# Layer 0's bias from the positional encoding, taken from the prompt's own compression

## The chip, the cores and the metric

The kernel runs on one core of a Trainium2 chip. The metric is the device time of one execution in microseconds; the time before is the median of three runs. Names of engines: PE is TensorE (PEld its weight loads), DVE is VectorE, ACT is ScalarE, POOL is GpSimd, SP is SyncE, which issues most DMAs.

## What is computed

One inference step of a decoder trunk of two layers, for one prompt of 256 new tokens and eight sequences with 8 new tokens and 1024 old ones each; all 320 tokens go through the same weights. A layer mixes tokens by three paths (a state-space path, a causal pooling, and sparse attention), projects, and runs a convolutional feed-forward block. The change lies in the sparse attention, where keys and values are compressed in blocks of 32 rows, 16 apart:

```python
def compress_blocks(rows, pe, w1, w2):
    ...
    ch = rows.reshape(b, n_ch, CMP_STRIDE, d)
    h = (jnp.einsum('bnld,lde->bne', ch[:, :-1] + pe[:CMP_STRIDE], w1[:CMP_STRIDE])
         + jnp.einsum('bnld,lde->bne', ch[:, 1:] + pe[CMP_STRIDE:], w1[CMP_STRIDE:]))
    return jax.nn.gelu(h) @ w2
```

The encoding `pe` adds the same vector of 128 numbers to every block, `sum over l, d of pe[l, d] * w1[l, d, :]`, once for keys and once for values. The kernel computes that vector once per layer and uses it as the bias of the Gelu. The prompt has 15 blocks per layer, the eight sequences have 63 each from their cache.

## The kernel before

The kernel is written with a framework that sorts the program: each engine executes its instructions in an order that is fixed when the program is built, from the instructions' priorities (their place in the program) and from when their inputs are ready in the framework's own plan. `later(n)` adds n to the priorities of what stands in it, so that it yields to others. At run time every engine takes its queue strictly as it is written, and waits by semaphores. Tiles come from pools with a fixed number of buffers; a tile is freed when its last reader is done.

Layer 0's mixing part is listed in `ORDER[0]`, one short name per stage, with `@n` for `later(n)`. Those that matter here: `lw` loads the weights of the compression (`w1`, two tiles of 128 x 2048, and `w2`, which also holds `pe` in the columns 128 to 159). `hP0` and `hP2` gather cache pages with 32 indirect DMAs that POOL issues. `eb` is `enc_bias`, the stage that is dropped. `pr` is `nsa_prep`, which transposes the prompt's keys, values and queries and compresses its 15 blocks. `x` is `xbc`, eight tiles of the input projection (24 matmuls `mt` each, weights split in two parts by ACT and DVE, results taken over by DVE into `ext`, edge columns copied to `ocv`). `c0` to `c3` compress the sequences' cache (`cs`).

`enc_bias` (line 834) takes `pe` as the stationary operand: 16 matmuls for keys and 16 for values, each of 32 stationary columns (only the first is wanted) against 128 columns of `w1`, in four groups of 32 partitions of the tile `pe`. Each is written in two passes in the trace. ACT copies the sums to `pes`, two small matmuls `hb` add up the four groups, and DVE copies the two columns to `c.hb`. Layer 1 runs the same stage in `feed`, between the layers.

`nsa_prep` compresses the prompt in the same manner. `pcl` holds the prompt's rows, 16 chunks for each of eight pairs of rows, for keys and values; 32 matmuls `pc` with 32 stationary columns each run against `w1`, into four groups of partitions. Of the 32 result rows 15 are used. DVE copies them to `pcs`; the matmuls `pf` add up the four groups with a constant (`FOLD`) and turn the result; ACT applies the Gelu with bias `c.hb` into `hc`; `ckp` and `cvp` apply the second weight. `cvp` needs `hpd`, a copy of `hc` that POOL makes.

Of the kernel before, what the change touches and what calls it, by code (L numbers as in the profile page):

```python
# [7 lines left out]
_o = 0  # L8
for _n, _w in (("ID", 128), ("ONE", 128), ("P", 1), ("TRI", 128), ("TRIU", 128), ("TRIS", 64), ("TRIUS", 64), ("GM", 128), ("SEL", 256), 
               ("CAU", 128), ("CMP", 32), ("HS", 12), ("NEW", 8), ("WOLD", 8), ("COS", 24), ("SIN", 24), ("RW", 2),  # L10
               ("IC", 32), ("FOLD", 15), ("J1", 14), ("BM", 4), ("B8", 8)):
    globals()["C_" + _n] = _o
    _o += _w
NCST = _o
# [11 lines left out]
def constants():  # L26
    f = np.float32
    c = np.zeros((128, NCST), f)
    p = np.arange(128)
    c[:, C_ID:C_ID + 128] = np.eye(128)  # L30
    c[:, C_ONE:C_ONE + 128] = 1
    c[:, C_P] = p
    c[:, C_TRI:C_TRI + 128] = p[:, None] <= p[None]
    c[:, C_TRIU:C_TRIU + 128] = p[:, None] > p[None]
    q = np.arange(64)
    same = q[:, None] // 8 == q[None] // 8
    c[:64, C_TRIS:C_TRIS + 64] = same & (q[:, None] <= q[None])
    c[:64, C_TRIUS:C_TRIUS + 64] = same & (q[:, None] > q[None])
    same_bq = (p[:, None] // 32 == p[None] // 32) & (p[:, None] % 8 == p[None] % 8)
    c[:, C_GM:C_GM + 128] = same_bq  # L40
    for g in range(2):
        b, h, i = p // 32 + 4 * g, p // 8 % 4, p % 8
        c[b * 8 + i, C_SEL + 128 * g + p] = 1
    c[:, C_HS:C_HS + 12] = (p // 8 % 4)[:, None] == np.arange(12)[None] // 3
    c[:, C_CAU:C_CAU + 128] = np.where(p[None] <= p[:, None], 0, NEG)
    for qt in range(2):
        m = np.where(16 * np.arange(16)[None] + 31 <= (qt * 128 + p)[:, None], 0, NEG)
        m[:, 15] = NEG
        c[:, C_CMP + 16 * qt:C_CMP + 16 * qt + 16] = m
    c[:, C_NEW:C_NEW + 8] = np.where(np.arange(8)[None] <= (p % 8)[:, None], 0, NEG)  # L50
    c[:, C_WOLD:C_WOLD + 8] = np.where(np.arange(8)[None] > (p % 8)[:, None], 0, NEG)
    half = 8
    inv = (1.0 / (f(500000.0) ** (np.arange(half, dtype=f) / f(half)))).astype(f)
    for j in range(3):
        pos = (p + 128 * j if j < 2 else 1024 + p % 8).astype(f)
        ang = (pos[:, None] * inv).astype(f)
        c[:, C_COS + 8 * j:C_COS + 8 * j + 8] = np.cos(ang)
        c[:, C_SIN + 8 * j:C_SIN + 8 * j + 8] = np.sin(ang)
    for g, w in enumerate((2, 4, 8, 16)):
        r = slice(64 * (g % 2), 64 * (g % 2) + 64)  # L60
        c[r, C_RW + g // 2] = f(1) / f(w)
        c[r, C_IC + 16 * (g // 2):C_IC + 16 * (g // 2) + 16] = f(w) / np.minimum(np.arange(16) + 1, w).astype(f)
    c[:, C_FOLD:C_FOLD + 15] = (p % 32)[:, None] == np.arange(15)[None]
    c[:, C_J1:C_J1 + 14] = np.arange(1, 15)
    c[:96, C_BM:C_BM + 4] = (p[:96] % 32)[:, None] // 8 == np.arange(4)[None]
    c[:64, C_B8:C_B8 + 8] = q[:, None] // 8 == np.arange(8)[None]
    return c
# [71 lines left out]
def post(o):  # L139
# [28 lines left out]

ORDER = ["lw hP0@500 hP2@500 eb@100 hS1@500 pr x hS3 st g c0@0 c1 p0 c2 c3@200 l0 o0 n0@200 p1 o1 s0 po n1@0 z l1 s1@0 r0@100 r1@100 ss",
         "pr n0 st l0@500 g@500 n1 p0 p1 z s0@0 o1 po r0 l1@500 o0 s1@100 x r1 ss"]  # L170


def build(ctx, tc, nc, A):
# [4 lines left out]
    F32, F32R, I32 = mybir.dt.float32, mybir.dt.float32r, mybir.dt.int32  # L178
    AF, OP = mybir.ActivationFunctionType, mybir.AluOpType
    X, XY = mybir.AxisListType.X, mybir.AxisListType.XY  # L180
    PE, DVE, ACT, POOL, SP = nc.tensor, nc.vector, nc.scalar, nc.gpsimd, nc.sync
# [35 lines left out]
    s1 = pool("s1", 1)  # L217
# [58 lines left out]
    cst = one.tile([128, NCST], F32, name="cst")  # L276
# [5 lines left out]
    def mm(out, l, r, start=True, stop=True):  # L282
        return PE.matmul(out, l, r, start=start, stop=stop, skip_group_check=True)  # L283
# [537 lines left out]
    def load_w1(c):  # L821
        c.w2 = s1.tile([128, 416], F32, name="w2", tag="w2")
        SP.dma_start(c.w2, A["w2"][c.l])
        ck = s1.tile([128, 4, 80], F32, name="ckT", tag="ckT")
        c.ckT = [ck[0:64], ck[64:128]]
        c.cvb = [s1.tile([80, 4, 64], F32, name="cvb", tag=f"cvb{g}") for g in range(2)]
        c.w1 = []
        for kv in range(2):
            w = w8_p.tile([128, 16, 128], F32, name="w1", tag="w8")
            SP.dma_start(w, A["w1"][c.l, kv].rearrange("p (k c) -> p k c", k=16))  # L830
            c.w1.append(w)
# [42 lines left out]
    def nsa_prep(c):  # L874
        l, kvn, qn = c.l, c.kvn, c.qn
        pcl = n2([128, 512], "pcl")
        POOL.memset(pcl[:, 256:288], 0.0)
        pv = pcl[:, 0:256].rearrange("p (i k c) -> p i k c", i=2, k=8)
        c.KT = KT = s1.tile([64, 528], F32, name="KT", tag="KT")
        c.qT = [n2([64, 4, 128], "qT") for _ in range(2)]  # L880
        kvd = n2([128, 2, 2, 2, 64], "kvd")
        qd = n2([64, 4, 2, 64], "qd")
        for u in range(2):
            ACT.activation(kvd[:, :, :, u], kvn[:, 0:2, 0:128].rearrange("p j (i d) -> p j i d", i=2), AF.Copy)
            DVE.tensor_copy(qd[:, :, u], qn[2][:64].rearrange("p (h d) -> p h d", h=4))
        for j in range(2):
            ps = nst("kT")
            for i in range(2):
                transpose(ps[:, 128 * i:128 * i + 128], kvd[:, j, i].rearrange("p u d -> p (u d)"))
            transpose(ps[:64, 256:384], kvn[:, j, 128:192])  # L890
            transpose(ps[:64, 384:512], kvn[:, j, 256:320])
            for i in range(2):
                for par in range(2):
                    r = slice(64 * par, 64 * par + 64)
                    v = ps[r, 128 * i:128 * i + 128].rearrange("p (c k u) -> p k c u", k=8, u=2)[:, :, :, par]
                    cp(f"pv{l}{j}{i}{par}", "A" if par else "D", pv[r, i, :, 8 * j:8 * j + 8], v)
            cp(f"KT{l}{j}", "A", KT[:, 272 * j:272 * j + 256], ps[:64, 256:512])
            ps = nst("qT")
            for h in range(4):
                transpose(ps[:64, 128 * h:128 * h + 128], qn[j][:, 64 * h:64 * h + 64])  # L900
            cp(f"qT{l}{j}", "A", c.qT[j], ps[:64].rearrange("p (h t) -> p h t", h=4))
        hc = n1("hc")[:, :64].rearrange("p (v k) -> p v k", v=2)
        POOL.memset(hc, 0.0)

        ps = nst("pc")
        for kv in range(2):
            for kk in range(16):
                r, c0 = 32 * (kk % 4), 128 * kv + 16 * (kk % 8) + kk // 8
                mm(ps[r:r + 32, 128 * kv:128 * kv + 128], pcl[:, c0:c0 + 32], c.w1[kv][:, kk], start=kk < 4, stop=kk > 11)
        pcs = d1("pcs")  # L910
        cp(f"pcs{l}", "D", pcs, ps[:, 0:256])
        ps = nst("pf")
        for kv in range(2):
            mm(ps[:, 16 * kv:16 * kv + 15], pcs[:, 128 * kv:128 * kv + 128], cst[:, C_FOLD:C_FOLD + 15])
            ACT.activation(hc[:, kv, 0:15], ps[:, 16 * kv:16 * kv + 15], AF.Gelu_apprx_tanh, bias=c.hb[:, kv:kv + 1])
        ps = nst("ckp")
        mm(ps[:64, 0:16], c.w2[:, 0:64], hc[:, 0, 0:16])
        DVE.tensor_copy(KT[:, 256:272], ps[:64, 0:16])
        ps = nst("cvp")
        hpd = n1("hpd").rearrange("p (h k) -> p h k", h=4)  # L920
        POOL.tensor_copy(hpd, hc[:, 1:2, :].to_broadcast([128, 4, 32]))
        mm(ps[:, 0:64], hpd.rearrange("p h k -> p (h k)"), c.w2[:, 64:128])
        c.cvd = s1.tile([128, 4, 64], F32, name="cvd", tag="cvd")
        POOL.memset(c.cvd, 0.0)
        for h in range(4):
            r = slice(32 * h, 32 * h + 32)
            DVE.tensor_copy(c.cvd[r, h], ps[r, 0:64])

        c.qsT = s1.tile([128, 8, 4, 8], F32, name="qsT", tag="qsT")
        ps = nst("qsT")  # L930
        for h in range(4):
            transpose(ps[:, 64 * h:64 * h + 64], qd[:, h].rearrange("p u d -> p (u d)"))
        ACT.activation(c.qsT.rearrange("p b h q -> p h b q"),
                       ps[:, 0:256].rearrange("p (h b q) -> p h b q", h=4, b=8), AF.Copy)
        c.nT = A_p.tile([128, 2, T], F32, name="nT", tag="A")
# [333 lines left out]
    c = params(0)  # L1269
# [61 lines left out]
```

## Time and profile before

| | |
|---|---|
| median of three runs | 1232.06 us (1231.94 to 1237.4) |
| the profiled execution | 1224.47 us, its span 1222.3 us |
| PE | 1171.7 us busy, 96% |
| DVE / ACT / POOL | 66% / 44% / 25% busy |
| granted clock of PE | 0.97 on average |

The span is the time from the first to the last instruction of the profiled execution. Layer 0's mixing part ends at about 235 us, its output projection at 265 us, its feed-forward block at 630 us; layer 1's mixing part lies between 650 and 815 us. A matmul's end is modelled, so neighbouring matmuls overlap in the listing: the distance from one start to the next is what a matmul costs.

### The profile page before, as it was taken

What the parts mean: (1) busy time and instruction counts of PE and PEld (TensorE: products, weight loads), DVE (VectorE), ACT (ScalarE), POOL (GpSimd) and SP (SyncE); (2) the same over time, 40 slices, a digit from 0 to 9 for tenths busy, and PEclk for the clock granted to TensorE, in tenths of its full rate; (3) what the DMA queues carried; (4) which work ended last, traced back from release to release, by engine and by line L of the source; (5) the groups of instructions that cost most, each with busy time, mean ns of one, the idle gap of its engine ahead of it and who ended that gap; (6) DMA issues with size and microseconds to landing.
All of it is one profiled execution on the core that took longest, in us unless ns stands there. A gap on an engine that the chain in (4) does not pass through costs nothing.

```text
span 1222.3 us, 23199 instructions
## 1 busy us (share of the span) xinstructions
PE 1171.7 (96%) x8450; PEld 1093.2 (89%) x8450; DVE 802.5 (66%) x1661; ACT 536.7 (44%) x950; POOL 302.5 (25%) x616
## 2 busy tenths in 40 slices
PE   7999998899999999999999999889999999999995
PEld 6799765599999999999999877778899999999995
DVE  4583667368756666656663688986685666666665
ACT  5445523236454444433433565433455444444431
POOL 4732222100513113311300033440342311111111
PEclk9999999699999999999999999898899999999998
DMA  7634227355555455545433445206345544445421
GB/s 277 191 100 137 76 85 252 100 161 185 175 177 199 167 168 181 159 146 184 156 104 105 154 131 189 99 27 199 119 138 171 165 143 159 152 145 158 150 72 43
DMA packets 85186, 180.18 MB, mean 147 GB/s; under 512 B 10449, under 2 KB 45009, under 8 KB 84049
## 3 DMA queue, kind: packets, MB, share of 16 engines
q1 hardware_dynamic: 84048, 176.61, 45.0%
q0 software_dynamic: 1024, 2.10, 0.6%
q8 instruction: 66, 1.08, 0.4%
q14 instruction: 48, 0.39, 0.1%
HBM read 168.97 MB, written 13.83 MB: 150 GB/s over the span
## 4 chain that ended last, share of the span: by engine, by line
PE 88%; DVE 5%; POOL 2%; ACT 2%; issue 1%; DMA 1%; SPq 1%; DVEq 0%; POOLq 0%; ACTq 0%
PE mt L283 67%; PE cs L283 5%; PE nat L283 4%; PE sn L283 1%; PE O L283 1%; PE sb L283 1%; PE sc L283 1%; PE yoh L283 1%; PE ss L283 1%; PE pe L283 1%; PE rb L283 1%; PE pT L287 1%; DMA h<-s_ssm 1%; PE sA L283 1%; DVE xt L437 1%
## 5 line engine op out<-in xcount | busy, mean ns | idle before, releaser
L342 ACT ACTIVATE wh<-raw 128x1024 fp32r<-128x1024 f32 (+2 forms) x156 | 159.9, 1026 | 199.7 <-PE mt L283 147.2
L283 PE MATMUL mt<-xh,wa 128*128 128x320 f32 x1024 | 237.2, 310 | 0.0
L283 PE MATMUL mt<-xl,wh 128*128 128x320 f32 x736 | 232.0, 315 | 0.0
L283 PE MATMUL mt<-xh,wl 128*128 128x320 f32 x736 | 231.2, 314 | 0.0
L283 PE MATMUL mt<-xh,wh 128*128 128x320 f32 x736 | 230.9, 315 | 0.2 <-ACT xh L421 0.2
L290 DVE TENSOR_TENSOR wl<-raw,wh 128x1024 fp32r<-128x1024 f32 (+2 forms) x151 | 179.5, 1189 | 68.2 <-ACT wh L342 65.5
L283 PEld LDWEIGHTS mt<-xh,wa 128*128 128x128 f32 x1024 | 174.8, 188 | 0.3
L283 PE MATMUL mt<-xl,wa 128*128 128x320 f32 x512 | 158.5, 310 | 0.0
L283 PEld LDWEIGHTS mt<-xh,wh 128*128 128x128 f32 x736 | 138.9, 189 | 5.8 <-issue 5.0
L283 PEld LDWEIGHTS mt<-xh,wl 128*128 128x128 f32 x736 | 138.8, 189 | 4.6 <-issue 3.9
L283 PEld LDWEIGHTS mt<-xl,wh 128*128 128x128 f32 x736 | 139.0, 189 | 3.2 <-issue 2.4
L290 DVE TENSOR_TENSOR wa<-raw,wa 128x1024 fp32r<-128x1024 f32 x92 | 113.5, 1234 | 37.2 <-ACT wa L342 36.9
L290 POOL TENSOR_TENSOR fa<-fa,fc 128x256 f32<-128x256 f32 (+1 forms) x128 | 82.0, 662 | 191.5 <-ACT fc L1171 136.8
L342 ACT ACTIVATE wa<-raw 128x1024 fp32r<-128x1024 f32 x92 | 96.8, 1053 | 48.4 <-DMA raw<-wg 34.9
L283 PE MATMUL mt<-act,wa 128*128 128x320 f32 x768 | 117.8, 309 | 0.0
L283 PEld LDWEIGHTS mt<-act,wa 128*128 128x128 f32 x768 | 114.0, 188 | 0.0
L283 PE MATMUL mt<-act,wh 128*128 128x320 f32 x512 | 113.2, 309 | 0.0
L283 PEld LDWEIGHTS mt<-xl,wa 128*128 128x128 f32 x512 | 96.3, 188 | 0.0
L1164 POOL COPY off<-fext 128x2 f32<-128x2 f32 x64 | 19.5, 304 | 283.2 <-DVE fext L290 283.2
L283 PEld LDWEIGHTS mt<-act,wh 128*128 128x128 f32 x512 | 85.6, 188 | 0.0
L290 DVE TENSOR_TENSOR fo<-fo,mt 128x320 f32<-128x320 f32 x112 | 54.0, 484 | 44.6 <-PE mt L283 44.3
L283 PE MATMUL mt<-act,wl 128*128 128x320 f32 x256 | 79.1, 309 | 0.0
(375 smaller groups left out, 1976.2 us busy)
## 6 DMA issues: line engine op xcount, KB each, us to landing
raw<-wg SPq DMA_DIRECT2D x168, 512.0 KB
raw<-wd SPq DMA_DIRECT2D x64, 512.0 KB
cache<-cslc SPq DMA_DIRECT2D x128, 64.0 KB
cache<-ccmp SPq DMA_DIRECT2D x96, 64.0 KB
w<-w SPq DMA_DIRECT2D x4, 1024.0 KB
o_sss<-h SPq DMA_DIRECT2D x16, 256.0 KB
o_winold<-wnat SPq DMA_DIRECT2D x16, 252.0 KB
raw<-wnb SPq DMA_DIRECT2D x8, 384.0 KB
```

Of the source, the lines that this page charges most:

```text
L283: return PE.matmul(out, l, r, start=start, stop=stop, skip_group_check=True)
L287: return PE.transpose(out, in_, ident[:k, :k])
L290: return eng.tensor_tensor(out, a, b, op)
L342: ACT.activation(h, src, AF.Copy)
L437: DVE.scalar_tensor_tensor(t, mixo[k], w(k), rb if k else pb, op0=OP.mult, op1=OP.mult)
L1164: POOL.tensor_copy(off[:, m % 8, 0:2], ext[:, 256:258])
```

## The change

In layer 0 the stage `eb` is dropped from the order. `pcl` gets 32 columns for each pair of rows in place of 16, is set to zero as a whole, and POOL copies the encoding from `w2` into its columns 16 and 17. The `pc` matmuls, as many as before, then compute the encoding's sum as a 17th result row. The fold takes 17 columns instead of 15. Where no bias is there yet (layer 0), DVE copies it out of the fold's result, and the two Gelus follow behind both folds. In layer 1 `enc_bias` still runs, and the 17th row is computed and not used.

```diff
-               ("IC", 32), ("FOLD", 15), ("J1", 14), ("BM", 4), ("B8", 8)):
+               ("IC", 32), ("FOLD", 17), ("J1", 14), ("BM", 4), ("B8", 8)):
...
-ORDER = ["lw hP0@500 hP2@500 eb@100 hS1@500 pr x hS3 st g c0@0 c1 p0 c2 c3@200 l0 o0 n0@200 p1 o1 s0 po n1@0 z l1 s1@0 r0@100 r1@100 ss",
+ORDER = ["lw hP0@500 hP2@500 hS1@500 pr x hS3 st g c0@0 c1 p0 c2 c3@200 l0 o0 n0@200 p1 o1 s0 po n1@0 z l1 s1@0 r0@100 r1@100 ss",
...
+        c.hb = None
...
         pcl = n2([128, 512], "pcl")
-        POOL.memset(pcl[:, 256:288], 0.0)
-        pv = pcl[:, 0:256].rearrange("p (i k c) -> p i k c", i=2, k=8)
+        POOL.memset(pcl, 0.0)
+        pv = pcl.rearrange("p (i k c) -> p i k c", i=2, k=8)
+        for i in range(2):
+            POOL.tensor_copy(pv[:, i, :, 16:18], c.w2[:, 128 + 16 * i:144 + 16 * i].rearrange("p (u k) -> p k u", u=2))
...
-                r, c0 = 32 * (kk % 4), 128 * kv + 16 * (kk % 8) + kk // 8
-                mm(ps[r:r + 32, 128 * kv:128 * kv + 128], pcl[:, c0:c0 + 32], c.w1[kv][:, kk], start=kk < 4, stop=kk > 11)
+                r, c0 = 32 * (kk % 4), 256 * kv + 32 * (kk % 8) + kk // 8
+                w = min(32, 512 - c0)
+                mm(ps[r:r + w, 128 * kv:128 * kv + 128], pcl[:, c0:c0 + w], c.w1[kv][:, kk], start=kk < 4, stop=kk > 11)
...
         for kv in range(2):
-            mm(ps[:, 16 * kv:16 * kv + 15], pcs[:, 128 * kv:128 * kv + 128], cst[:, C_FOLD:C_FOLD + 15])
-            ACT.activation(hc[:, kv, 0:15], ps[:, 16 * kv:16 * kv + 15], AF.Gelu_apprx_tanh, bias=c.hb[:, kv:kv + 1])
+            mm(ps[:, 18 * kv:18 * kv + 17], pcs[:, 128 * kv:128 * kv + 128], cst[:, C_FOLD:C_FOLD + 17])
+        if c.hb is None:
+            c.hb = s1.tile([128, 2], F32, name="hb", tag="hb")
+            DVE.tensor_copy(c.hb, ps[:, 16:36:18])
+        for kv in range(2):
+            ACT.activation(hc[:, kv, 0:15], ps[:, 18 * kv:18 * kv + 15], AF.Gelu_apprx_tanh, bias=c.hb[:, kv:kv + 1])
```

## Rows read from the trace of the kernel before

**Rows 1.** The page's engine totals: busy us, share of the span, instructions.
```profile
PE 1171.7 (96%) x8450; PEld 1093.2 (89%) x8450; DVE 802.5 (66%) x1661; ACT 536.7 (44%) x950; POOL 302.5 (25%) x616
```

**Rows 2.** Busy time by stretch: length, PE, PEld, DVE, ACT, POOL, clock, DMA share, GB/s.
```profile
60.00:65.00 5.00, 3.72 (x22) 3.30 (x22) 2.68 (x8) 1.60 (x3) 2.70 (x8) 0.87 0.24 67
65.00:70.00 5.00, 5.00 (x32) 5.00 (x32) 4.27 (x10) 2.17 (x5) 1.13 (x1) 0.79 0.28 96
...
130.00:140.00 10.00, 10.00 (x50) 6.80 (x50) 8.97 (x26) 2.30 (x6) 8.26 (x12) 1.00 0.40 118
...
220.00:230.00 10.00, 4.84 (x14) 2.16 (x14) 1.68 (x3) 1.26 (x2) 1.55 (x2) 0.50 0.24 79
230.00:240.00 10.00, 10.00 (x58) 8.85 (x57) 5.56 (x24) 2.40 (x8) 0.55 (x2) 0.78 0.30 88
```

**Rows 3.** Timeline of PE around the dropped stage: start us, us, instruction.
```profile
37.86 0.41 PE L283 MATMUL pe<-w,w 128*32 128x128 f32 x2
38.19 0.42 PE L283 MATMUL mt<-xh,wl 128*128 128x320 f32 x1
...
38.87 0.41 PE L283 MATMUL mt<-xh,wh 128*128 128x320 f32 x1
...
46.69 1.28 PE L283 MATMUL pe<-w,w 128*32 128x128 f32 x34
47.90 0.42 PE L283 MATMUL mt<-xh,wh 128*128 128x320 f32 x1
...
49.94 0.28 PE L283 MATMUL hb<-cst,pes 128*128 128x1 f32 x2
```

**Rows 4.** PE's timeline: prompt's compression, a later gap; brackets: idle before, its releaser.
```profile
54.08 1.95 PE L283 MATMUL pc<-w,pcl 128*32 128x128 f32 x64
...
57.59 0.36 PE L283 MATMUL pf<-cst,pcs 128*128 128x15 f32 x2 [0.64 <-DVE an L556]
...
59.79 0.29 PE L283 MATMUL pf<-cst,pcs 128*128 128x15 f32 x2
...
62.50 0.43 PE L283 MATMUL cvp<-w,hpd 128*128 128x64 f32 x2 [1.28 <-POOL hpd L921]
...
227.00 1.92 PE L283 MATMUL yoh<-h,csp 128*32 128x256 f32 x4 [5.16 <-DMA h<-s_ssm]
```

**Rows 5.** Timeline of POOL, from the start to the copy hpd.
```profile
1.43 0.13 POOL L877 MEMSET pcl<- 128x32 f32 x1
...
18.68 0.10 POOL L328 MEMSET ms<- 128x3 f32 x1 [4.43 <-DVE rt L305]
18.96 1.18 POOL L469 DMA_INDIRECT cache<-ccmp,idx  x1 [0.17 <-issue]
...
59.95 0.94 POOL L469 DMA_INDIRECT cache<-ccmp,idx  x1 [0.30 <-issue]
...
61.12 0.52 POOL L196 COPY ocv<-ext 128x3 f32<-128x3 f32 x1
...
62.16 0.28 POOL L921 COPY hpd<-hc 128x128 f32<-128x128 f32 x1
...
84.65 0.21 POOL L196 COPY ocv<-ext 128x24 f32<-128x24 f32 x1 [2.29 <-DVE ext L290]
```

**Rows 6.** The chain that ended last, in order of time: start us, us, what.
```profile
68.55 17.01 PE mt L283 x116
```

**Rows 7.** Timeline of DVE: the second tile's weights, the first tile's result, the old bias.
```profile
37.39 1.28 DVE L290 TENSOR_TENSOR wl<-raw,wh 128x1024 fp32r<-128x1024 f32 x1
...
46.80 0.56 DVE L290 TENSOR_TENSOR ext<-mt,rb 128x256 f32<-128x256 f32 x2 [5.42 <-PE mt L283]
...
52.52 0.14 DVE L846 COPY hb<-hb 128x2 f32<-128x2 f32 x1
```

**Rows 8.** Timeline of SP: the load of w2.
```profile
9.16 0.33 SPq L823 DMA_DIRECT2D w<-w  x1
```

**Rows 9.** Timeline of POOL in layer 1, ahead of the copy hpd there.
```profile
689.81 0.29 POOL L290 TENSOR_TENSOR anb<-an,cst 64x64 f32<-64x64 f32 x1 [28.49 <-DVE an L556]
```

More of the change, by code (lines that the diff above doesn't have):

```diff
@@ L62, in constants @@
         c[r, C_IC + 16 * (g // 2):C_IC + 16 * (g // 2) + 16] = f(w) / np.minimum(np.arange(16) + 1, w).astype(f)
-    c[:, C_FOLD:C_FOLD + 15] = (p % 32)[:, None] == np.arange(15)[None]
+    c[:, C_FOLD:C_FOLD + 17] = (p % 32)[:, None] == np.arange(17)[None]
     c[:, C_J1:C_J1 + 14] = np.arange(1, 15)
```

## The prediction

> **What bounds the kernel now.** I read four views, in this order. The engine totals say that TensorE (PE) is occupied for 96% of the span and POOL for a quarter [rows 1]; a kernel like this gains where PE's own work shrinks, and only there. The table by stretch then says where that is true: from 70 us to 140 us PE has no idle time in any row (the last one stands there), and the last stretch of layer 0 before the output projection (220 to 230 us) is no longer a matter of PE work, as PE is occupied there for 4.84 of 10 us [rows 2]. Third, PE's own timeline around the stage that is dropped [rows 3], and around the prompt's compression that takes the work over [rows 4]. Last, POOL's queue, because one PE instruction behind the compression waits for POOL [rows 4, 5]. The reader should see two things. The dropped stage lies in PE's queue with no gap, so its time is PE time. And POOL's queue is closed from 18.96 us to 60.89 us by 32 gathers that are issued one by one every 1.25 us [rows 5].
>
> **The removed stage.** The 64 records of `pe` (32 matmuls of 32 columns, two passes each) lie between 37.86 us and the `hb` at 49.94 us, and are interleaved with the x tiles' matmuls `mt`: 13 times one `mt` and one pair of `pe`, then 34 records of `pe` in a row, then two more pairs [rows 3]. An `mt` in an undisturbed row costs 17.01/116 = 0.147 us [rows 6]. One step of the interleaving, from one `mt` to the next, takes 38.87 - 38.19 = 0.68 us, so a pair costs 0.68 - 0.147 = 0.53 us; in a row, 34 records take 1.21 us (46.69 to 47.90), 0.036 us each. The stage's price on PE is 15 pairs x 0.53 + 1.21 = 9.2 us. The two visits of `hb` are listed with 0.28 us, which overlaps their neighbours; I take half, 0.14 us each. Sum removed: 9.5 us. The copy `pes` on ACT and the old `hb` copy on DVE go too; DVE idles for 5.42 us in this stretch, until the first x tile is ready [rows 7], and ACT waits for the same tile, so they count as nothing. Layer 1 keeps its stage.
>
> The Trainium skill, TensorEngine Tiling (Array Packing), section Tiling Modes, says that narrow tiles run side by side, but that a change of tiling mode drains the engine. By the first half alone the stage would be worth 64 x 0.036 = 2.3 us, by both halves some 9 us; the rows agree with both halves.
>
> **What takes its place on PE.** The compression of the prompt already issues 32 stationary blocks of 32 columns (`pc`, 64 records, 1.95 us) [rows 4]. Rows 16 of these blocks were computed before and thrown away; filled with the encoding they cost nothing more. The last block is 31 columns wide; nearest rows are the 32-column ones, so 0, at most one switch (0.53 us). The fold is 17 columns for 15: 0. Both folds now stand before both Gelus: before, the second fold waited for the first Gelu, 2.2 us behind the first one [rows 4]. The new copy of the bias stands between fold and Gelu on DVE: 0.14 us by its own old row [rows 7] and one handover more. So this chain is as long as before, within 1 us on either side, and I take 0.
>
> **POOL.** The memset of `pcl` grows from 32 to 512 columns: 0.13 us becomes at most 16 times that, 2.1 us; it stands at 1.43 us, and the gathers can't start before the instruction at 18.68 us, ahead of which POOL has 4.43 us of idle time: 0 [rows 5]. The two new copies have 16 columns each; copies of 24 and of 3 columns take 0.21 and 0.52 us, so both cost 0.4 to 1.0 us; I take 0.5 us, nearer to the row with more columns. Their input, the load of `w2`, is issued at 9.16 us [rows 8], and POOL's idle time ahead of 18.68 us comes behind that [rows 5]: there they cost nothing. If the order puts them between the gathers, the gathers end 0.5 us later. I take 0.3 us. In layer 1 POOL is idle for 28.49 us ahead of that place [rows 9]: 0, unless something on PE is reordered there (bounds -1 and +1 us).
>
> **Where the freed 9.5 us go.** Behind the compression stands `cvp`, which waits for POOL's copy `hpd` [rows 4]. `hpd` runs at 62.16 us, directly behind the gathers [rows 5]. It isn't late by its input: even the copy of the first x tile's edge (`ocv`), whose input was ready at 47.36 us [rows 7], stands behind all 32 gathers. `hpd` needs the chain kT, pcl, pc, pf, hc, which the order sets after that first tile, so I expect it to stay behind the gathers. The gathers start after an instruction that waits for the first norm (18.68 us) and do not depend on the dropped stage. So `cvp` stays at 62.5 us, plus the 0.3 us. PE gains only as far as it has done other work before `cvp`.
>
> That other work is x tiles. The second tile's matmuls begin at 47.90 us, though their weights were split by 38.67 us [rows 3, 7]. And the 34 `pe` records in a row stand exactly between the last `mt` of one tile and the first of the next: some 17 instructions of the program lie between these two, and 17 `pe` matmuls were merged in, one per place. So the order is made by place in the program, not by lack of work, and a place that `pe` leaves is taken by an `mt`. With one `mt` for each of the 32 `pe` matmuls, PE has 32 x 0.147 = 4.7 us of later work done when it stands before `cvp`, and 9.5 - 4.7 = 4.8 us are given back as a longer wait there (1.28 us before). Both ends stay for the range: no `mt` more (0 gained) and all of 9.5 us.
>
> **The clock.** Around the 1.28 us before `cvp` the granted clock falls: the stretches 60 to 65 and 65 to 70 us have 0.87 and 0.79, a mean of full speed (2.4 GHz) and the lower of the two levels (1.2 GHz) [rows 2, 4]. That costs 5 x 0.13 + 5 x 0.21 = 1.7 us. Behind the 5.16 us gap at 227 us [rows 4] the clock is at 0.50 up to 230 us and 0.78 in the 10 us after it [rows 2]: (230 - 227) x 0.5 + 10 x 0.22 = 3.7 us. A wait of some 6 us before `cvp` thus costs between -1.7 us (no fall) and 3.7 - 1.7 = 2.0 us more than before; I take 1.0 us, nearer to the second row as its gap is nearer.
>
> The Trainium skill, TensorE: Matmul & The Clock Gate, section Why this matters for your kernels, says that idle gaps between bursts of matmuls bring the clock back to its lower level. Here that speaks against the change, and the trace agrees at both places named.
>
> **The sum.** -9.5 + 4.8 + 1.0 + 0.3 = -3.4 us, against a profiled span of 1222.3 us in an execution of 1224.47 us. From 70 to 140 us PE has no idle time, so what it has done before is passed on; the chain behind, with its waits for loads [rows 4], starts from that work and moves with it. The runs shown have a median of 1232.06 us, 7.6 us above the profiled execution; I take the difference over to the median: 1228.7 us.
>
> **Rivals.**
> (a) Everything passes: `hpd` is placed among the gathers, or the x tiles fill all of the hole. Against it stands POOL's order [rows 5], for it the five us of idle time on DVE, which leave room for the tiles' follow-up work [rows 7]. -9.5 us, 1222.6 us.
> (b) Nothing passes: the order merely loses `pe`, and PE waits some 11 us before `cvp`, with the clock's full price. +0.3 + 2.0 = +2.3 us, less up to 1 us for shorter folds: 1233 to 1234.4 us. For it: POOL is closed until 60.9 us in any case. Against it: the tiles that are ready.
> (c) Slower: the copies of the encoding are placed behind the gathers. Then `pcl` is complete at 61.5 us, not before 54.08 us, and `pc` starts 7.4 us later; from `pc` to `cvp` PE needed 8.4 us, of which 0.64 + 1.28 us were waits that would go: +7.4 - 1.9 + 1.0 (clock) = +6.5 us with no tile moved up, +1.8 us with 32 `mt`. It decides at the place: once more than about 20 of the 32 gathers (18.96 + 20 x 1.25 = 44 us) stand ahead of the copies. Against it: `w2` is issued ten us before the first gather. 1234 to 1238.6 us.
>
> **How the numbers follow.** Forecast (half passes) 0.47, with its own range 1224.5 to 1231.5 us; (a) 0.18; (b) 0.22; (c), with whatever else a new order of the list may spoil in layer 0, 0.13. Half a per cent, about what a measurement of this kernel can tell from no change, is 6.2 us, so the line for faster is 1225.9 us: (a) and about a quarter of the forecast's chance, 0.30. Slower needs 1238.2 us: 0.13 as the upper end of (c) and of unknown orders. The rest, 0.57, is within. The range leaves out a part of (c) and what lies below (a) with 1.5 us for the folds: 1221 to 1237 us.
>
> **What would show it.** Right: no `pe` in layer 0; first x tile of 24 `mt` in one run of 3.5 us from 36 us on; more than 39 `mt` between that and `cvp`; `cvp` near 62.5 us with an idle time of several us by `hpd`; a clock below 1 for some us after it; from 70 us on every stage 3 to 4 us early. Wrong: `hpd` before 60 us on POOL (a); PE idle for 10 us before `cvp` (b); L877's copies behind the gathers (c). The whole reading fails if the stretch from 146 to 235 us changes its length, since then the order there, not the removed work, makes the difference.

## The result, and the profile after

The changed kernel is slower: 1241.26 us (median of 17 runs, 1238.23 to 1243.31) against 1231.77 us (17 runs beside them, 1222.45 to 1239.24), a ratio of 1.0093 with an interval of [1.0071, 1.0115]. That is 9.5 us between the medians and some 11 us by the ratio, and outside the range of the prediction. Repeated in another comparison (e13 below) it was 1.0074 [1.0044, 1.0104]. Executions that take over 1.5% longer than the fastest of their kernel are left out of every ratio here (three of e1's twelve, one of e4's six). The profiled execution of the changed kernel took 1242.38 us (span 1240.6 us). It stands 18 us above the one of before, some 6 us more than the ratio says, as the one of before was among its kernel's fastest; so the profiles tell where time goes, and the ratios how much it is.

The page's engine totals answer to [rows 1]: 68 PE records fewer, and 95% for 96%.

```profile
PE 1174.8 (95%) x8382; PEld 1099.0 (89%) x8382; DVE 804.1 (65%) x1661; ACT 535.7 (43%) x949; POOL 300.8 (24%) x620
```

PE's timeline of the changed kernel around the prompt's compression (start us, us, instruction, idle time before it and its releaser), against [rows 3, 4]:

```profile
45.84 1.95 PE L283 MATMUL pc<-w,pcl 128*32 128x128 f32 x64
...
48.91 0.59 PE L283 MATMUL pf<-cst,pcs 128*128 128x17 f32 x4 [0.18 <-DVE s__1307 L290]
...
51.57 0.29 PE L283 MATMUL ckp<-hc,w 128*64 128x16 f32 x2
...
64.03 0.69 PE L283 MATMUL cvp<-w,hpd 128*128 128x64 f32 x2 [11.53 <-POOL hpd L929]
```

The compression comes 8 us earlier, costs what it did, and then PE stands for 11.53 us where it stood for 1.28. POOL's timeline shows why; it answers to [rows 5]:

```profile
20.01 0.10 POOL L328 MEMSET ms<- 128x3 f32 x1 [4.42 <-DVE rt L305]
20.05 0.35 POOL L881 COPY pcl<-w 128x16 f32<-128x16 f32 x2
20.58 1.18 POOL L469 DMA_INDIRECT cache<-ccmp,idx  x1 [0.17 <-issue]
...
61.65 0.94 POOL L469 DMA_INDIRECT cache<-ccmp,idx  x1 [0.30 <-issue]
...
63.68 0.29 POOL L929 COPY hpd<-hc 128x128 f32<-128x128 f32 x1
```

`hpd` still stands behind all 32 gathers. The Trainium skill, PSUM — Partial Sum Buffer, section Engine vs sequencer instructions, says that GpSimd's queue is strictly first in, first out; the trace agrees, as `hpd` needs 0.29 us and runs behind the last gather, while with the copy on DVE (e1 below) `cvp` runs at 51.74 us.

But this isn't all. PE's busy time by stretch (length, PE, PEld, DVE, ACT, POOL, clock, DMA share, GB/s), against [rows 2]:

```profile
60.00:65.00 5.00, 0.97 (x5) 0.86 (x6) 0.23 (x2) 0.00 (x0) 3.21 (x9) 0.50 0.16 48
65.00:70.00 5.00, 5.00 (x23) 4.88 (x22) 3.67 (x9) 2.05 (x6) 0.57 (x2) 0.50 0.30 90
70.00:75.00 5.00, 5.00 (x34) 5.00 (x34) 3.20 (x10) 1.18 (x2) 0.00 (x0) 0.90 0.28 84
...
140.00:150.00 10.00, 8.87 (x49) 7.18 (x48) 7.08 (x26) 5.39 (x21) 1.41 (x3) 1.00 0.34 122
150.00:160.00 10.00, 6.16 (x23) 5.37 (x24) 6.50 (x17) 4.64 (x13) 3.22 (x4) 0.66 0.21 59
...
230.00:240.00 10.00, 5.56 (x22) 3.55 (x22) 2.58 (x4) 1.26 (x2) 2.33 (x3) 0.74 0.28 90
240.00:250.00 10.00, 10.00 (x44) 8.84 (x44) 4.65 (x22) 2.40 (x8) 0.55 (x2) 0.58 0.34 103
```

Just before 150 us a new hole begins, with a fallen clock behind it. The list of what PE waited for up to 300 us (total us, times, longest) names it:

```profile
PE cvp L283 <- POOL hpd L929: 11.5, 1, 11.5
...
PE pct L287 <- POOL Pc L290: 4.7, 1, 4.7
PE yoh L283 <- DMA h<-s_ssm: 4.3, 1, 4.3
...
PE yd L283 <- DVE xdt L290: 1.9, 1, 1.9
```

In the kernel before, the second `pct` (it transposes the prompt's attention weights) waited 0.9 us for POOL. The orders of the two programs say what happened: before, 35 matmuls of later tiles and the state-space part's first `dec` stood between the last `kn` (a transpose of new rows) and the second `pct`; now 11 matmuls do, and the first `dec` comes at 176.9 us, behind the sample scores `sC` (from 166.7 us). PE's timeline before, two lines, and after:

```profile
147.72 1.05 PE L283 MATMUL dec<-cst,G 128*128 128x128 f32 x8
...
149.78 0.33 PE L287 MATMUL pct<-cst,Pc 128*128 128x128 f32 x1 [0.90 <-POOL Pc L290]
```

```profile
153.60 0.48 PE L287 MATMUL pct<-cst,Pc 128*128 128x128 f32 x1 [4.74 <-POOL Pc L290]
```

The planner, which sorts by its own idea of when things are ready, has dealt the instructions differently over a large part of layer 0.

The lag of the changed kernel can be read off the tiles' first and last starts. The table is put together from the rows that the trace gives for single tiles on PE, in us; the experiments of the next section are in it already. The columns follow PE's work through layer 0: `cvp`, the compression `cs` of the cache's pages, `cks` (its second weight, for keys), the prompt's `pct`, the state-space path's `yd`, and the output projection's `mt`.

| | first cvp | first cs | first cks | first pct | last yd | first mt of output projection | pct to yd |
|---|---|---|---|---|---|---|---|
| before | 62.5 | 66.0 | 91.1 | 124.7 | 192.6 | 235.2 | 67.9 |
| changed | 64.0 | 68.9 | 94.6 | 129.2 | 205.7 | 244.2 | 76.5 |
| changed, again (e13) | 63.6 | 68.2 | 92.9 | 127.5 | 203.5 | 241.9 | 76.0 |
| e1: hpd on DVE | 51.7 | 64.1 | 90.3 | 124.9 | 201.7 | 242.5 | 76.8 |
| e2: before, hpd on DVE | 61.5 | 63.4 | 88.1 | 121.7 | 189.5 | 238.8 | 67.8 |
| e3: changed, stage kept | 63.1 | 67.0 | 92.3 | 125.9 | 193.7 | 236.3 | 67.8 |
| e4: before, stage left out | 63.4 | 68.0 | 93.7 | 128.3 | 205.0 | 244.4 | 76.7 |
| e14: hpd and pages | 52.8 | 55.3 | 86.2 | 120.9 | 197.2 | 236.9 | 76.3 |
| e17: gathers mixed in | 51.6 | 54.1 | 81.4 | 116.3 | 192.3 | 230.8 | 76.0 |
| e15: o1 delayed | 63.3 | 67.7 | 92.4 | 130.4 | 197.3 | 238.6 | 66.9 |
| e16: hpd, pages, o1 | 53.1 | 55.6 | 86.6 | 124.6 | 190.5 | 231.8 | 65.9 |
| e18: mixed in, o1 | 52.8 | 55.3 | 84.0 | 121.9 | 189.0 | 230.3 | 67.1 |

Two rows of tiles from which the last column comes (time range of one, count, first and last start), of the kernel before:

```profile
L287 PE MATMUL pct<-cst,Pc x2: 278/303/328, 124.7 to 149.8; 128*128 128x128 f32 x2
L283 PE MATMUL yd<-G,xdt x48: 218/272/324, 164.3 to 192.6; 128*64 128x128 f32 x32, 64*64 64x64 f32 x16
```

and of the changed one:

```profile
L287 PE MATMUL pct<-cst,Pc x2: 279/378/476, 129.2 to 153.6; 128*128 128x128 f32 x2
L283 PE MATMUL yd<-G,xdt x48: 218/272/323, 184.1 to 205.7; 128*64 128x128 f32 x32, 64*64 64x64 f32 x16
```

At the last `mt` of the output projection the changed kernel is 10.9 us behind (275.9 us for 265.0), and 9.7 us in e13 (274.7): about what the ratios say of the whole.

### The profile page after: what moved, and what is told of

Same layout as the page of the kernel before. It is cut to its first block, busy times and chain, and to the rows that moved or that the text cites. A ratio compares the mean times of both kernels' runs of the same rounds, so it can differ in the third digit from the quotient of the medians.

```text
span 1240.6 us, 23084 instructions
## 1 busy us (share of the span) xinstructions
PE 1174.8 (95%) x8382; PEld 1099.0 (89%) x8382; DVE 804.1 (65%) x1661; ACT 535.7 (43%) x949; POOL 300.8 (24%) x620
## 4 chain that ended last, share of the span: by engine, by line
PE 86%; DVE 5%; POOL 3%; issue 2%; ACT 2%; DMA 1%; SPq 0%; DVEq 0%; POOLq 0%; ACTq 0%
PE mt L283 66%; PE cs L283 5%; POOL cache L469 3%; PE nat L283 2%; PE sb L283 1%; PE O L283 1%; PE sc L283 1%; PE sn L283 1%; PE dec L283 1%; PE ss L283 1%; PE sA L283 1%; PE Os L283 1%; PE rb L283 1%; PE pT L287 1%; DVE cv L581 1%
## 5 line engine op out<-in xcount | busy, mean ns | idle before, releaser
L290 POOL TENSOR_TENSOR fa<-fa,fc 128x256 f32<-128x256 f32 (+1 forms) x128 | 77.8, 628 | 190.3 <-ACT fc L1179 133.5
L290 DVE TENSOR_TENSOR fo<-fo,mt 128x320 f32<-128x320 f32 x112 | 54.1, 484 | 45.4 <-PE mt L283 45.2
```

What stands on the lines that cost most here:

```text
L290: return eng.tensor_tensor(out, a, b, op)
```

## The experiments

The edits are few, and each has a letter. H takes `hpd` off POOL in layer 0; P puts the second list of gathers behind the first; M lets the second list be asked for behind `x`; O delays the second half of the prompt's attention in the planner's priorities:

```diff
H  -        POOL.tensor_copy(hpd, hc[:, 1:2, :].to_broadcast([128, 4, 32]))
   +        (POOL if l else DVE).tensor_copy(hpd, hc[:, 1:2, :].to_broadcast([128, 4, 32]))
P  -ORDER[0]: lw hP0@500 hP2@500 hS1@500 pr x ...
   +ORDER[0]: lw hP0@500 hP2@1500 hS1@500 pr x ...
M  +ORDER[0]: lw hP0@500 hS1@500 pr x hP2@500 ...
O  -ORDER[0]: ... p1 o1 s0 ...
   +ORDER[0]: ... p1 o1@50 s0 ...
```

The runs fell on several chips. In the first comparison, and on the three chips of e1 to e4, e13 to e16, and e17 and e18, the kernel before has medians of 1228 to 1232 us; on the one of e5 to e12, called the slower chip here, it has 1260 to 1262 us, because there PE reaches `cvp` only at 82 to 95 us. Each ratio is to the kernel before on the same chip. Medians are compared directly only within one comparison.

### The stop before cvp, and the layout: e1 to e4

e1 is the changed kernel with H, e2 the kernel before with H. e3 is the changed kernel with `eb@100` put back into the order; e4 is the kernel before without it, with `c.hb` set to zero by DVE in layer 0, so that it leaves the encoding out of layer 0's compression.

> The changed kernel with one copy moved in layer 0: hpd goes from POOL, where it stands behind the 32 gathers, to DVE. The order of PE is that of the changed kernel but for one matmul. Theory 'wait': the 11.5 us that PE stands before cvp, and the fall of the clock behind it (about 3 us), are the loss. PE then stands there for less than 1 us, the clock stays at 1.00 over most of 60 to 75 us, and the time is 14 us under the changed kernel's 1241: 1227 (1224 to 1231), that is the 9.5 us of the dropped stage come through. Theory 'order': the wait is made good by 95 us (only 3.5 us of lag stood there in the profiled run), and the loss comes from the new order behind 140 us and from layer 1. Then the gain at cvp is mostly lost again behind it, and the time stays at 1235 or more.

> The kernel before with the same move of hpd to DVE: the control. PE stood 1.3 us before cvp there. Theory 'wait': 1.3 us are gained, some more with the clock: 1229 to 1232. Theory 'order': nothing, 1232. Both: under 3 us; more would say that DVE's place for the copy is worth something of its own.

> The changed kernel with the bias's own stage put back in layer 0, so that the bias comes from it and the 17th row's column is computed but not used there: the new layout, its memset and its copies alone, with PE's order behind cvp nearly that of the kernel before. Theory 'layout' (the copies in front of the gathers, the whole memset, the joint fold and the start cost the 10 us): 1238 to 1243. Theories 'wait' and 'order': within 2 us of the kernel before, 1230 to 1234, with PE standing 1 to 3 us before cvp.

> The kernel before with the bias's stage left out in layer 0 and nothing put in its place: the bias there is zero, so the positional encoding's part of the compression is left out of layer 0. The old layout, and PE's order nearly that of the changed kernel. Theories 'wait' and 'order': as slow as the changed kernel, 1238 to 1243, with PE standing some 11 us before cvp, though the chip has 49 matmuls less to do. Theory 'layout': 1222 to 1232.

Measured: e1 1.0096 [1.0053, 1.0139]; e2 0.9975 [0.9940, 1.0010]; e3 1.0018 [0.9982, 1.0054]; e4 1.0103 [1.0035, 1.0171].

The layout is cleared of the bulk of the loss: with all the new columns and copies, but the stage kept, e3 agrees with the kernel before in the ratio, and in every column of the table within 1.2 us. It isn't cleared of all: the interval leaves room for half a per cent, and layer 1 takes 3.0 us longer in e3's profile (see the next section). And leaving out 34 matmuls of the program (68 records, not the 49 of the expectation), with nothing in their place, makes e4 as slow as the changed kernel, though its times lie far apart, three at 1235 to 1239 us and three at 1253 to 1254 us. Its profile, one of the latter, has the changed kernel's waits in layer 0 (11.4 us at `cvp`, 4.7 us at the second `pct`) and its column of 76.7 us. So it is the absence of the stage that costs.

My first theory, that the wait for `hpd` is the loss, fell with e1: PE passes `cvp` at 51.7 us without waiting, 9.8 us before e2, and the ratio is what it was (the two kernels didn't run side by side, and the interval leaves room for a gain of some 5 us). PE's timeline of e1:

```profile
51.74 0.33 PE L283 MATMUL cvp<-w,hpd 128*128 128x64 f32 x2
52.00 0.46 PE L287 MATMUL qsT<-cst,qd 64*128 64x64 f32 x4
...
64.10 2.48 PE L283 MATMUL cs<-cache,w 128*128 128x128 f32 x10 [9.69 <-DMA cache<-ccmp,idx]
```

The next stop stood right behind the first: `cs`, the compression of the cache's pages, waits 9.69 us for the gathered pages, and starts 2.7 us after the last gather began at 61.35 us. `cs` reads only the first list (16 pages), which at 1.25 us each from 19.84 us on could be there by 43 us, an estimate. But as the program was built, POOL issues five pages of the first list, then 15 of the second (needed at `c2`, far later), and the other eleven of the first list among the last twelve. The trace doesn't tell the two lists apart; what it shows is that `cs` waits for the end of the gathers here, and no longer does in e14, where the first list is gathered first. The Trainium skill, Perfetto Trace Analysis, section DMA Instruction — SWDGE (GPSIMD), says that the end that is shown of such a DMA is the end of writing its descriptors and not of the transfer; the trace agrees: the last gather's record ends at 62.29 us, and `cs` starts 1.8 us behind it.

### The pages: e5, e6, e9, e13, e14

e5, e9 and e14 are one kernel: changed, H and P. e6 is the kernel before with H and P.

> As e1 (the changed kernel, hpd on DVE), and the second list of 16 gathers of layer 0 (for c2) made to stand behind the first list (for c0); the planner had put 11 of c0's 16 last. PE's order is that of e1. In e1 PE passed cvp at 51.7 us and then stood 9.7 us before the first cs, until 64.1, for the last gather's pages. Theory 'gathers': that wait bounds the stretch, and the dropped stage can't show before it is gone: now cs starts at 54 to 55 us, the first pct at 115 to 117 instead of 124.9, and the time is 10 us (8 to 13) under e1's 1237 to 1239.5: 1228 (1225 to 1231). The new order behind 125 us keeps costing its 8 us. Rival 'next wait': the hT memsets, which stay behind all 32 gathers on POOL, or the loads of the x weights hold PE instead; then pct comes at 121 or later and the time stays over 1234.

> The kernel before with the same two edits (hpd on DVE, c0's pages gathered first): the control of e5. PE has the bias's stage to do, reaches cvp at about 61.5 us and cs at about 63.5 and finds nothing to wait for. Theory 'gathers': 0 to 1 us under e2's 1226.6: 1225 to 1228, as the stage's 9.5 us lay in the shade of the gathers there. If e6 gains as much as e5 did over e1 (10 us), the gathers cost the kernel before too, and the theory is wrong.

> The kernel of e5 once more. On the chip of e5 to e8 the loads of the second projection's weights came so late that PE stood some 25 us before it had done it, and reached cvp at 84 to 94 us, when the 32 gathers were long over; what they hold up could not show there. On a chip where PE is at cvp by 52 us (e1): theory 'gathers': cs starts at 54 to 55 us instead of 64.1, the first pct is 8 to 10 us earlier than in e1 (115 to 117), and the time is 0.4% or more under e1's ratio of 1.0096 to the kernel before. Rival 'weights': in e5 the 8 us that were gained at cvp were gone by the first pct, lost in a wait for the z weights at 120 to 130 us. If that wait is there on this chip too, cs starts at 54 but the first pct is at 122 or later, and the ratio stays at 1.006 to 1.010.

> The changed kernel itself, beside e14 to e16 on one chip. Where PE is at cvp at 52 us: ratio 1.007 to 1.011 as in the first comparison. Where the second projection's weights come 25 us late (the chip of e5 to e12), PE passes cvp without a stop at 84 to 86 us; theory 'order': what is gained there is lost behind it as in e5 and e9 (same order), ratio 1.002 to 1.006. If the stop at cvp were all of the loss, the ratio there would be 0.992 to 0.996.

> hpd on DVE and c0's pages first, the changed kernel's order. Where PE is at cvp at 52 us: theory 'gathers' has cs at 54 to 55 us and the first pct at 115 to 117, ratio 1.000 to 1.004; rival 'weights' has the first pct at 122 or later, 1.006 to 1.010. On the chip with the late weights the two edits have nothing to remove: the ratio is that of e13 within 0.3%.

Measured: e5 1.0030 [0.9995, 1.0065], e6 0.9988 [0.9949, 1.0028], e9 1.0045 [1.0015, 1.0076], all on the slower chip; in one comparison on another, e13 1.0074 [1.0044, 1.0104] and e14 1.0009 [0.9975, 1.0043], that is 1242.11 and 1232.23 us.

Beside e13 the two edits together are worth 9.9 us, where H alone (e1, on another chip) gave nothing that its ratio could show. P alone was not run. `cs` starts at 55.3 us as expected, but the first `pct` comes at 120.9 us, not at 115 to 117: of the 12.9 us that `cs` has gained over e13, 6.7 are left at the first `cks`. The list of waits of e14 between 50 and 75 us has the third stop of the same kind:

```profile
ACT cv L579 <- POOL ocv L196: 6.4, 1, 6.4
...
PE mt L283 <- DVE ext L290: 3.3, 1, 3.3
```

ACT's work on an x tile waits for POOL's small copies `ocv`, which stand behind the last gather too; DVE waits for ACT, and PE for DVE.

On the slower chip, PE passes `cvp` at 85.2 us in e5 and 93.8 us in e6, both without a wait, as the gathers are over by 62 us: the dropped stage's 8.6 us come through. At the first `cks` they are still there (112.4 and 120.4 us), at the first `pct` they are gone (153.8 and 154.0 us). Between these two, PE waited 3.1 us for the split of weights that ACT in turn had waited 2.6 us for, until they were loaded; and the clock fell (e5, busy time by stretch):

```profile
120.00:130.00 10.00, 6.86 (x33) 4.86 (x32) 2.40 (x6) 4.16 (x7) 3.38 (x5) 0.73 0.79 262
130.00:140.00 10.00, 10.00 (x65) 9.02 (x65) 4.18 (x22) 5.94 (x26) 0.30 (x1) 0.76 0.20 57
```

3.1 us idle and 20 us at 0.73 to 0.76 make 8.2 us (3.1 + 10 x 0.27 + 10 x 0.24): all of the gain. So there a different resource, the loads, holds the same stretch. The changed kernel itself was not run on the slower chip.

### The order: e7, e10, e12, e15

e7, e10 and e15 are one kernel: changed, O alone. e12 is the kernel before with O.

> The changed kernel with one number in its order: o1 with a delay of 50 in the planner's priorities in layer 0, so that the ssd's first dec and xn stand ahead of the second pct on PE again, much as in the kernel before, in place of after the sample scores. hpd and the gathers are left as they are. Theory 'order': the lag of the changed kernel does not grow from 4.5 us at the first pct to 13 at the last yd; it stays at 4 to 6 us up to the output projection, and the time falls by 5 to 8 us: 1233 to 1236. Theory that the wait at cvp, with its clock, is all: still 1239 to 1243.

> The kernel of e7 once more, for the same reason. Theory 'order': the stop at cvp (11.5 us) is still there, and the lag of the changed kernel stays at 4 to 6 us from the first pct to the output projection instead of growing to 9 and more; ratio to the kernel before 1.001 to 1.005. If the stop at cvp and the clock behind it are all of the loss: 1.008 to 1.011.

> o1 delayed by 50, hpd and gathers as in the changed kernel. Theory 'order': 0.3 to 0.8% under e13 on either chip. If the order is worth nothing: the same as e13 within 0.3%.

> The kernel before with the same one number (o1 delayed by 50), with the bias's stage kept: how much a new order by itself is worth. There the first dec still stands ahead of the sample scores, but behind the second pct, and PE's order differs from the kernel before in some 380 places behind cvp. Theory 'order': the time turns on where the ssd's first dec stands; it is early here, so within 0.4% of the kernel before. If any new order costs, as the one tuned by hand is lost: 1.004 to 1.010.

Measured: e7 1.0008 [0.9978, 1.0039] and e10 1.0033 [1.0004, 1.0063] on the slower chip; e15 1.0040 [1.0009, 1.0071], that is 1235.46 us against 1242.11 us of e13 beside it; e12, on the slower chip, 1.0105 [1.0050, 1.0160].

One number in a priority list gives 6.7 us back, with the stop of 11.5 us before `cvp` still there. The table's last column is 67.8 to 67.9 us wherever the order of the kernel before stands (before, e2, e3; 67.8 in e6), and 76.0 to 76.8 wherever the changed kernel's stands (with or without the stops in front of it; 79 in e5 and e9). PE has nearly the same matmuls in that stretch in both groups (538 and 536 records of the same tiles). With O the column says too much: its 66 to 67 us hold 23 matmuls of later tiles fewer, which have moved ahead of the first `pct` (38.0 us behind the first `cks` in e15, 34.6 in e13). From the first `cks` to the last `yd` the work is the same again; PE's busy time of before, e13 and e15 there:

```profile
91.10:192.60 101.50, 98.07 (x805) 79.40 (x806) 58.04 (x174) 46.85 (x125) 28.46 (x44) 1.00 0.38 118
```

```profile
92.90:203.50 110.60, 102.93 (x805) 81.72 (x805) 60.84 (x173) 47.44 (x124) 27.91 (x44) 0.97 0.38 119
```

```profile
92.40:197.30 104.90, 98.34 (x804) 80.62 (x805) 56.24 (x172) 46.71 (x124) 26.79 (x44) 0.97 0.39 120
```

So O gives back 5.7 of the 9.1 us, and only 1.1 us of that is idle time (7.7 and 6.6 us), though the wait at the second `pct` falls from 4.7 to 0.8 us; others, of 1.5 and 1.2 us, take its place. The rest is PE's busy time for the same matmuls.

For the changed kernel, the 8.6 us more from the first `pct` to the last `yd` are made up of 3.8 us more idle time in all (7.2 for 3.4; the second `pct` alone waits 3.8 us more) and about 3.1 us of clock behind it (the 6.4 us up to 160 us at 0.52): 6.9 us. What can hold the rest: counted in the traces, the stationary block changes its size (128, 64 or 32 rows or columns) 73 times in this stretch, for 63 times before. A change costs between 0.09 us (0.24 us from the start of an `mt` to that of a smaller block, for 0.147 us to another `mt`) and 0.23 us (half of the pair's 0.53 us in the prediction, less its records), so ten more are 0.9 to 2.3 us, an estimate. With O there are 11 changes fewer than in e13 from the first `cks` to the last `yd` (77 for 88; before, 76), which by the same estimate explains 1.0 to 2.5 of its 4.6 us of busy time; the rest is open. Some four of the 8.6 us are made good up to the output projection, where `yoh` waits 4.3 us in place of 6.7.

e12 shows that this isn't a matter of where the first `dec` stands alone, as I had it: there it stands early, the last column is 68.5 us, and the kernel is 1% slower all the same, with the stage kept and no other edit. Here too 23 matmuls have moved ahead of the first `pct`, and the last column hides the loss: from the first `cks` to the last `yd` it is 105.4 us, for 101.4 in e6, with 2.9 us more idle time. What e12 loses otherwise is open. No run has the order of the kernel before with only the stage taken out; that the new order costs is shown, but not what the same change would have been worth with the old one.

### Both, and a queue that is open: e8, e11, e16, e17, e18

e8, e11 and e16 are one kernel: changed with H, P and O. e17 is changed with H and M, e18 is e17 with O.

> The changed kernel with all three: hpd on DVE, c0's pages gathered first, o1 delayed by 50. 'Gathers' and 'order' together: 10 us from the one and 5 to 8 from the other, 1220 to 1226, under the kernel before. If the two are one and the same loss seen twice, 1228 to 1232.

> The kernel of e8 once more (hpd on DVE, c0's pages first, o1 delayed by 50). 'Gathers' and 'order' together: ratio 0.990 to 0.996, under the kernel before. Rival 'weights': what the first two edits gain is lost to the z weights before the first pct, and it is e10's ratio, 1.000 to 1.005.

> All three edits. Where PE is at cvp at 52 us: 0.990 to 0.996, if the stop and the order add; 1.000 to 1.005 if what the stop gives back is lost to the weights. On the chip with the late weights: as e15 within 0.3%, 0.998 to 1.003.

> As e14, but the second list of gathers is asked for behind x in the program, so that POOL issues them in four lots between the ocv copies and the hT memsets, and not all ahead of these. PE's order is exactly that of e14. Theory 'gathers': ACT's 6.4 us for the ocv copies and PE's 3.3 us behind them are gone, the first cks comes at 81 to 83 us instead of 86.2, the first pct at 116 to 118 instead of 120.9, and the ratio to the kernel before falls from 1.001 by 0.3% or more: 0.995 to 0.998. Rival: another wait, for the x weights or for DVE, takes the place; the first cks stays at 85 or later and the ratio at 1.000 to 1.002. Where the second projection's weights come 25 us late, none of this can show, and the ratio is that of e5 and e9.

> As e17 with o1 delayed by 50 (e16's order). 'Gathers' and 'order': 0.2 to 0.5% under e16's 0.9986, that is 0.993 to 0.997 and under the kernel before. Rival: the stretch behind 130 us is bound by its own chain (the state loads h, the sample scores), which does not start earlier by the same amount: within 0.2% of e16.

Measured: e8 1.0015 [0.9982, 1.0047], e11 0.9988 [0.9954, 1.0022], e16 0.9986 [0.9955, 1.0018] (1229.08 us); e17 1.0016 [0.9986, 1.0046] (1231.32 us), e18 0.9966 [0.9937, 0.9994] (1225.55 us against 1231.76).

The stops and the order are two losses, though they don't add fully: from 1242.1 us (e13) the stops give 9.9, the order 6.7, both 13.0 (e14 to e16, beside it). e17 lets POOL do its small work between the gathers. Its timeline:

```profile
48.00 0.38 POOL L855 MEMSET hT<- 128x320 f32 x1
48.55 0.95 POOL L469 DMA_INDIRECT cache<-ccmp,idx  x1 [0.17 <-issue]
...
52.02 0.43 POOL L196 COPY ocv<-ext 128x3 f32<-128x3 f32 x2
52.60 0.97 POOL L469 DMA_INDIRECT cache<-ccmp,idx  x1 [0.15 <-issue]
...
65.74 0.94 POOL L469 DMA_INDIRECT cache<-ccmp,idx  x1 [0.30 <-issue]
66.68 0.50 POOL L196 COPY ocv<-ext 128x24 f32<-128x24 f32 x3
```

With PE's order unchanged from e14, the first `cks` comes at 81.4 us as expected, 9.7 us ahead of the kernel before and 6.7 us ahead of e2, which has H too: here most of the dropped stage shows at last. ACT's wait for `ocv` is halved (3.1 us), PE's behind it is 2.5 us. The lead over the kernel before is 8.4 us at the first `pct` and 0.3 us at the last `yd`: the order takes it. The ratio that I expected to fall by 0.3% didn't: e17 and e14, on two chips, can't be told apart, as each kernel's runs scatter by 6 to 8 us. e18, with O, is the only version below the kernel before whose interval leaves 1 out, by 0.34% (0.06 to 0.63%): that is 4 us, less than half of what the stage costs on PE, and less than the half per cent that I took as the limit of what can be told. It is 0.2% under e16, the line between the expectation and its rival, and on another chip, so it decides neither. Nor is it shown that the 4 us come from the dropped stage: the kernel before with H and M was not run.

## Why the prediction was wrong

**The removed stage, -9.5 us: right.** With H on both sides PE is at `cvp` 9.8 us earlier without the stage (51.7 and 61.5 us), on the slower chip, with P as well, 8.6 us (85.2 and 93.8).

**What takes its place on PE, 0: right.** `pc` has the same 1.95 us; from `pc` to `ckp`, which reads the first Gelu's result, it was 5.93 us (54.08 to 60.01 us) and is now 5.73 us.

**POOL, +0.3 us: right.** The two copies took 0.35 us together, directly ahead of the gathers; from the `ms` memset to the first gather it is 0.57 us, and was 0.28 us [rows 5]. The memset itself started 1.3 us later in the first profile, which I had not foreseen; in the profiles here it starts at 18.5 to 19.5 us with the old layout and at 19.1 to 20.0 us with the new one, so about half a microsecond goes with the layout and the rest is scatter.

**Where the freed time goes, +4.8 us: the first step that failed.** The mechanism was right: `hpd` stays behind the gathers and PE waits for it. The size was wrong: the wait grew by 10.2 us (11.53 for 1.28), not by 4.8, as 37 matmuls of x tiles stand between the first tile and `cvp`, where there were 39 and I expected 32 more. I had read the merged rows of `pe` as one place for one place. In fact the planner moved `pc`, `pf` and `ckp` up by 8 us and left the tiles where they stood relative to `cvp`; and with `hpd` on DVE it changes PE's order by a single matmul, so the gathers in front of `hpd` weigh next to nothing in its plan. This is rival (b), with its wait of some 11 us.

**A wait that the argument didn't have.** I took `cvp` to be the only thing that the gathers hold. `cs` was another: it started at 66.02 us in the kernel before, and by e1's interval of 2.7 us from the last gather's start its pages were there at 59.95 + 2.7 = 62.7 us [rows 5]. So 3.4 us was the most that could have passed even with `hpd` free. No row of before shows it, as a wait that is over in time leaves no idle time; the list of which instruction reads what POOL's queue delivers would have.

**The clock, +1.0 us (-1.7 to +2.0): about right.** Busy at 0.50 from 64.03 to 70 us and at 0.90 to 75 us costs 3.5 us, 1.8 us more than the 1.7 of before; in e13 `cks` has only 0.7 us more lag than `cvp`.

**"The chain behind starts from that work and moves with it": the step that decided.** It doesn't: the stretch from the first `pct` to the last `yd` grew from 67.9 to 76.5 us by a new order, with nearly the same matmuls in it. From rival (b)'s upper end, 1234.4 us, to 1241.26 us it is 6.9 us, and O alone gave 6.7 us back; that the two are so near is partly luck, as O is not the old order and layer 1 has a part in it too. The prediction named it as the sign of failure and gave such orders a place in (c), but it had no price for them, and the trace of before shows none.

**Layer 1, 0 (-1 to +1 us): too small, and not explained.** The 17th row's layout is in layer 1 too. In the profiles of before, e2, e6 and e12, with the old layout, PE is at the first `cvp` there 16.8 us after its second projection (the last `nat`), and needs 80.5 us from there to the last `Os`, the attention over the cache; in those with the new one, e3 among them, it is 15.3 and 83.1 to 83.2 us. So 1.5 us are gained and 2.7 lost, in whatever way layer 0 went. (e4, the fifth with the old layout, has 16.8 and 92.5 us; its clock from 712 to 805 us is 0.85.) From the last `nat` to the end of layer 1's output projection it is 167.1 to 167.2 us with the old layout in those four and 167.9 to 170.3 us with the new one, 170.1 in e3. Which part of the layout does it wasn't tried: no kernel had it in one layer alone.

## What to carry to other kernels

Work that is taken from an engine shows only up to the next thing that doesn't depend on it. Ask which queue delivers at a fixed time (here 32 gathers on POOL, issued from 19 to 61 us), and list everything that stands behind or reads from it, waits that are now zero included: here there were three in a row, and removing the first alone gained nothing that the runs could show. And where a planner deals out the instructions, removing some of them is also a new order: compare the two orders before the times, and measure an edit together with a neighbour that keeps the order (e3) or the work (e12).

## What the runs showed of the hardware

The clock fell while PE was listed as busy. In the profile of e2, 190 to 210 us, PE is busy in all of both stretches, at a mean granted clock of 0.67 and 0.65 (between its two levels, 2.4 and 1.2 GHz); the last idle time ahead of them is 0.9 us before a `yd` at 188.9 us:

```profile
190.00:200.00 10.00, 10.00 (x69) 5.38 (x68) 5.14 (x14) 0.76 (x3) 0.00 (x0) 0.67 0.46 167
200.00:210.00 10.00, 10.00 (x129) 6.44 (x128) 4.89 (x9) 1.79 (x5) 3.52 (x6) 0.65 0.48 157
```

In the kernel before, with nearly the same order and 3 us later, the same wait of 0.9 us lies inside the first stretch (`yd` at 192.1 us), and the clock is the full one:

```profile
190.00:200.00 10.00, 9.10 (x121) 5.57 (x110) 7.29 (x18) 2.96 (x8) 1.42 (x1) 1.00 0.72 249
200.00:210.00 10.00, 8.93 (x139) 6.16 (x138) 7.76 (x17) 3.48 (x9) 5.72 (x9) 1.00 0.62 196
```

That costs some 7 us (10 x 0.33 + 10 x 0.35), about as much as lies between the groups in which the runs of the kernel before fall (near 1225, 1232 and 1238 us). That it makes these groups isn't shown, and why it happens in some executions isn't known.

The slower chip differs in how SP's loads get on beside the gathers. SP's timeline of the kernel before in the first comparison, six loads of weights issued in 13.56 us:

```profile
25.46 13.56 SPq L347 DMA_DIRECT2D raw<-wg  x6
```

and of e6 on the slower chip, six in 45.70 us:

```profile
25.48 45.70 SPq L347 DMA_DIRECT2D raw<-wg  x6
```

In e6 the third of these is issued at 60.79 us, 30 us behind the second, when the last gather's record has ended (58.82 us). The gathers are issued at the same 1.25 us on both. The difference of some 30 us between the chips is there in full at PE's start of `cvp` (61.5 and 93.8 us in e2 and e6), and stays.
